# One-core encoder layer on Trainium2: full-tile operand sums go from GpSimd to VectorE, and the reciprocal roots become a multiply-add and a power on GpSimd

## The chip, the cores and the metric

The kernel runs on one core of one Trainium2 chip. The metric is the device time of one execution in microseconds (us). The engines of the core are named as in the profile: PE is TensorE (matrix products and transposes), DVE is VectorE, ACT is ScalarE, POOL is GpSimd, SP is SyncE, which issues most of the DMAs. Each engine works through its own list of instructions strictly in order.

## What is computed

One layer of an encoder on x of 1024 x 1024, float32. The parts that matter here, cut from the reference:

```python
h = rms_norm(x, g_mix)                       # x * rsqrt(mean(x*x) + eps) * g
z = h @ w_in                                 # queries, keys, values, index keys, gates
k_i = apply_rope(rms_norm(ik, g_idx_k))      # index keys; q_i has rope alone
y_a, y_b, y_c = band_attention, top-k sparse attention, gated recurrence
merged = sum over 3 branches of sigmoid(gate) * (y_branch @ w_branch)
x = x + merged @ w_out                       # out-projection
gu = rms_norm(x, g_ffn) @ w_ffn_in           # FFN-in
g_, u_ = split(gu)
x = x + (silu(g_) * u_) @ w_ffn_out          # FFN-out
```

Every product is made with float32 accuracy, so its operands are split in two parts, high and low.

## The kernel before

**Products.** `split` (L104 to L106) makes a high part with an ACT copy (L105) and the low part as raw minus high with a DVE subtraction (L106, names that end in l: `hl`, `ol`, `tql`, `fwl`). `mm3` (L121 to L123) then issues three matmuls: high by high, high by low, low by high. So a product can't finish before DVE has the low part of its operand.

**Seven products for eight.** The gate projection, the out-projection and both FFN products are made with a scheme that needs seven block products in place of eight. The price is sums and differences of operand blocks before the products. These are the full-tile operand sums of the change: 128x512 or 128x1024, two inputs in SBUF, output in SBUF. Before the change some of them stand on DVE and some on POOL:

- the index stage (about 20 to 90 us): `t2` of the rope on the queries, two 128x512 products on POOL for each half of the rows (L284, L285);
- the T stage (about 595 to 640 us), sums `tq` of the blocks of h for the gate projection: L796 to L800, of which two blocks of four (`ON_POOL`) and one low part are on POOL; the weights' sums of the same scheme are L872 to L875, and L889 adds two results;
- the comb stage (about 811 to 860 us), operand sums of the out-projection: L945 in `comb`, called from `o_prep`, 12 of 128x1024 on POOL, 4 on DVE;
- trans2 (about 920 to 947 us), sums of the normalised blocks for FFN-in: L1045 and L1047 on DVE, L1046 and L1048 on POOL;
- FFN-in (to about 1330 us): four 128x512 weight sums on POOL for each of 22 steps (L1169 to L1172).

**Reciprocal roots.** `rsqrt` (L125 to L140) makes 1/sqrt(scale * s + eps) on a narrow column by a bit trick and three Newton steps. It is 12 small instructions on DVE (the first norm in three batches, L184 to L187; the second norm, 8 tiles, L1002 to L1005) or 15 on POOL (index keys `rsk`, 128x4, twice, L274 to L278; heads of attention, `r16`, 128x16, eight times, L348 to L352).

**Order.** The Python code writes the work stage by stage, interleaved by hand (a string of letters decides which piece of attention comes between which products). The tile scheduler then sets the order of every engine's list by its own estimate of times, so moving an instruction to another engine also changes what stands around it. Loads for the FFN (`fa`, `fb`) are issued by SP; a load waits until the buffer that it overwrites is read for the last time. POOL also issues the DMAs that write intermediate results to DRAM.

```python
def split(raw, hi, lo, eng=None):
    S.activation(hi, raw, AF.Copy)
    (eng or V).tensor_tensor(lo, raw, hi.bitcast(F32), op=OP.subtract)
...
def comb(dst, a, op, b, eng=G):
    for o, x_, y_ in zip(dst, a, b):
        eng.tensor_tensor(o, x_, y_, op=op)
```

Of the kernel before, what the change touches and what calls it, by code (L numbers as in the profile page):

```python
# [20 lines left out]
D = 1024  # L21
# [14 lines left out]
ON_POOL = ('12', '21')  # L36
NPS = 0
# [45 lines left out]
def hybrid_kernel(ctx: ExitStack, tc: tile.TileContext, x, small, cs, bias_a, lru_w, w_idx, w_zg, w_c, w_g, w_b,  # L83
# [170 lines left out]
    for g in range(2):  # L254
# [29 lines left out]
        G.tensor_mul(t2[:, :, :, 0:32], zq[:, :, :, 32:64], bc(st[:, :, 0:32], 4))  # L284
        G.tensor_mul(t2[:, :, :, 32:64], zq[:, :, :, 0:32], bc(st[:, :, 32:64], 4))  # L285
# [115 lines left out]
    def attention(i, b0, pr, qk, v, mask, yT, isB=False):  # L401
# [4 lines left out]
        for e in range(2):  # L406
# [10 lines left out]
            (G if (b0 == 0 and isB and e < NPS) else V).tensor_scalar(P[:, 0:w], P[:, 0:w], rc, None, op0=OP.mult)  # L417
# [366 lines left out]
    def steps_T():  # L784
        tmp = Slots(arena, sl.free_list[:4])
        sl.free_list = sl.free_list[4:]
        for kp in range(2):
# [78 lines left out]
    def steps_W():  # L866
        for j in range(NPAIR):
# [21 lines left out]
            G.tensor_tensor(x, x, y, op=OP.add)  # L889
# [273 lines left out]
    def ffn_rest(j):  # L1163
# [313 lines left out]
```

## Time and profile before

| | us |
|---|---|
| median of 3 runs | 1560.23 (1556.93 to 1562.47) |
| the profiled execution, its time | 1559.64 |
| its span | 1557.9 |
| PE busy | 1485.1 (95%) |
| DVE busy | 1128.8 (72%) |
| ACT busy | 760.5 (49%) |
| POOL busy | 356.6 (23%) |

Busy shares are means over stages with different limits. In most of the span PE has no idle time; its roughly 70 us of idle time lie in a few stretches, and so the views by time (the windows, the timeline) tell more than the shares. In the timeline's rows a time in brackets is how long the engine was idle before the instruction and what ended that idle time. An instruction on DVE or POOL may show as busy while it waits for access to SBUF; its row is then longer than that of the same shape elsewhere.

### The profile page before, as it was taken

Reading aid. Unit: us, or ns where it says so; the run is one execution under the profiler, and the core shown is the slowest. Engines: PE = TensorE matmul, PEld = TensorE weight load, DVE = VectorE, ACT = ScalarE, POOL = GpSimd, SP = SyncE. Lnnn points to the kernel's source line nnn. Section 1 sums busy time; section 2 is a strip of 40 time slices with the busy share of each in tenths; the row PEclk is TensorE's granted clock in tenths of the full one; section 3 lists DMA queues with packets and bytes.
Section 4 is the critical chain, followed back from the end, with each engine's and each line's share of the span. In section 5 each row is a group of like instructions: output and inputs, shape, how many; then the busy total and the mean of one; then the engine's idle time right before and its main releaser. Section 6 shows DMA issues by size and latency. Waiting matters only on the chain. (4 is left out here: it accounts for less than half of the span.)

```text
span 1557.9 us, 20304 instructions
## 1 busy us (share of the span) xinstructions
PE 1485.1 (95%) x7612; PEld 1239.6 (80%) x7612; DVE 1128.8 (72%) x1932; ACT 760.5 (49%) x1188; POOL 356.6 (23%) x418
## 2 busy tenths in 40 slices
PE   6899989999999997999997988999999999999998
PEld 5888678889778875788885867888888888878887
DVE  5679999889666779748879887555555555378873
ACT  5455768865778665534213373333333333254440
POOL 1430001210000215542026153333333334000000
PEclk9999999999999999999998999999999999999999
DMA  4011212122111130348642231233333233598532
GB/s 173 28 45 42 68 37 88 57 82 78 54 45 55 41 109 28 135 155 291 231 152 105 95 109 41 95 108 103 114 96 113 98 121 117 217 360 293 187 128 88
DMA packets 51091, 178.43 MB, mean 115 GB/s; under 512 B 5872, under 2 KB 6000, under 8 KB 50992
## 3 DMA queue, kind: packets, MB, share of 16 engines
q1 hardware_dynamic: 36576, 128.36, 24.7%
q0 software_dynamic: 12688, 45.62, 7.5%
q10 hardware_dynamic: 1728, 3.15, 0.5%
q8 instruction: 60, 0.98, 0.3%
q14 instruction: 39, 0.32, 0.1%
HBM read 131.75 MB, written 45.35 MB: 114 GB/s over the span
## 5 line engine op out<-in xcount | busy, mean ns | idle before, releaser
L122 PE MATMUL B<-hl,fwh 128*128 128x512 f32 x528 | 207.1, 393 | 8.7 <-DVE hl L106 8.7
L121 PE MATMUL B<-hh,fwh 128*128 128x512 f32 x528 | 203.0, 391 | 1.6 <-ACT h2r L1023 1.6
L123 PE MATMUL B<-hh,fwl 128*128 128x512 f32 x528 | 199.7, 392 | 0.3 <-DVE fwl L106 0.3
L122 PEld LDWEIGHTS B<-hl,fwh 128*128 128x128 f32 x528 | 99.9, 189 | 30.7 <-DVE hl L106 10.0
L121 PEld LDWEIGHTS B<-hh,fwh 128*128 128x128 f32 x528 | 99.8, 189 | 22.7 <-ACT h2r L1023 1.8
L123 PEld LDWEIGHTS B<-hh,fwl 128*128 128x128 f32 x528 | 99.8, 189 | 21.2 <-DVE fwl L106 0.5
L122 PE MATMUL G<-wzl,hTh 128*128 128x256 f32 x384 | 111.0, 290 | 3.9 <-DVE wzl L106 3.9
L121 PE MATMUL G<-wzh,hTh 128*128 128x256 f32 x384 | 109.6, 287 | 2.0 <-ACT wzh L105 1.3
L123 PE MATMUL G<-wzh,hTl 128*128 128x256 f32 x384 | 110.0, 287 | 0.0
L122 PE MATMUL B<-fol,foh 128*128 128x512 f32 x264 | 102.8, 390 | 0.4 <-DVE fol L106 0.4
L123 PE MATMUL B<-foh,fol 128*128 128x512 f32 x264 | 101.9, 389 | 0.0
L121 PE MATMUL B<-foh,foh 128*128 128x512 f32 x264 | 101.1, 390 | 0.4 <-ACT foh L105 0.4
L106 DVE TENSOR_TENSOR fwl<-s,fwh 128x1024 fp32r<-128x1024 f32 x44 | 53.8, 1224 | 63.0 <-PE B L122 60.5
L660 ACT ACTIVATE junk_s<-score,ngS 128x1024 int8<-128x1024 f32 (+2 forms) x78 | 77.6, 995 | 21.1 <-DVE ngS L658 17.3
L122 PEld LDWEIGHTS G<-wzl,hTh 128*128 128x128 f32 x384 | 74.2, 193 | 5.4 <-DVE wzl L106 4.4
L123 PE MATMUL G<-hTh,wgl 128*128 128x512 f32 x192 | 76.3, 397 | 2.0 <-DVE wgl L106 2.0
L121 PEld LDWEIGHTS G<-wzh,hTh 128*128 128x128 f32 x384 | 74.0, 194 | 3.7 <-ACT wzh L105 1.7
L121 PE MATMUL G<-hTh,wgh 128*128 128x512 f32 x192 | 76.7, 400 | 0.0
L122 PE MATMUL G<-hTl,wgh 128*128 128x512 f32 x192 | 75.9, 395 | 0.0
L1188 DVE TENSOR_TENSOR act<-act,B 128x512 f32<-128x512 f32 x22 | 15.1, 688 | 82.2 <-PE B L123 82.2
L123 PEld LDWEIGHTS G<-wzh,hTl 128*128 128x128 f32 x384 | 74.3, 193 | 0.4 <-issue 0.2
L105 ACT ACTIVATE fw<-fb 128x512 fp32r<-128x512 f32 x22 | 13.9, 634 | 123.0 <-PE B L123 121.7
(499 smaller groups left out, 4146.1 us busy)
## 6 DMA issues: line engine op xcount, KB each, us to landing
fw<-in_w_fo SPq DMA_DIRECT2D x33, 512.0 KB, 5.9
fa<-pd SPq DMA_DIRECT2D x33, 512.0 KB, 5.0
gl<-gd SPq DMA_DIRECT2D x24, 512.0 KB, 5.8
fa<-in_w_fi SPq DMA_DIRECT2D x22, 512.0 KB, 3.5
fb<-in_w_fi SPq DMA_DIRECT2D x22, 512.0 KB, 3.9
pd<-act POOLq DMA_DIRECT2D x22, 512.0 KB, 6.1
ga<-in_w_g SPq DMA_DIRECT2D x18, 512.0 KB, 3.6
x<-in_x SPq DMA_DIRECT2D x12, 512.0 KB, 4.4
```

What stands on the lines that cost most here:

```text
L105: S.activation(hi, raw, AF.Copy)
L106: (eng or V).tensor_tensor(lo, raw, hi.bitcast(F32), op=OP.subtract)
L121: PE.matmul(o, lhsT=lh, rhs=rh, start=first, stop=False, **kw)
L122: PE.matmul(o, lhsT=lh, rhs=rl, start=False, stop=False, **kw)
L123: PE.matmul(o, lhsT=ll, rhs=rh, start=False, stop=last, **kw)
L660: S.activation(junk_s[:, 0:(i + 1) * 128], score[i], AF.Sign, bias=self.ng.bitcast(F32)[:, j:j + 1], accum_out=self.cnt[:, j:j + 1])
L1188: V.tensor_add(a1, a1, x)
```

## The change

It does three things. All the sums listed above, and the low part of T1, go from POOL to DVE. `rsqrt` becomes two POOL instructions, a multiply-add and a power with the exponent -0.5, for all its callers, those that had it on DVE too. The switches that no longer decide anything are taken out. The columns' exponents come from a 128x16 constant that DVE fills once. POOL's list goes from 417 to 162 instructions; the rest are DMAs, tables and memsets. In the changed file the lines up to `rsqrt` stand 2 lower, and those behind it 10 to 12 lower (L106 is L104, L796 is L784, L945 is L933, L1045 is L1033).

```diff
-    def rsqrt(dst, src, n, scale, eng=None):
-        E = G if eng is None else eng
+    mhalf = const.tile([128, 16], F32, name="mhalf")
+    V.memset(mhalf, -0.5)
+
+    def rsqrt(dst, src, n, scale):
         v = const.tile([128, n], F32, name="rs_v", tag=f"rsv{n}", bufs=2)
...
-        E.tensor_scalar(v, src, scale, EPS, op0=OP.mult, op1=OP.add)
-        E.tensor_scalar(y.bitcast(I32), v.bitcast(I32), -0.5, float(0x5F3759DF), op0=OP.mult, op1=OP.add)
-        E.tensor_scalar(v, v, -0.5, None, op0=OP.mult)
-        for it in range(3):
-            E.tensor_tensor(t, y, y, op=OP.mult)
-            E.tensor_tensor(t, t, v, op=OP.mult)
-            if E is V:
-                V.scalar_tensor_tensor(dst if it == 2 else y, t, 1.5, y, op0=OP.add, op1=OP.mult)
-            else:
-                G.tensor_scalar(t, t, 1.5, None, op0=OP.add)
-                G.tensor_tensor(dst if it == 2 else y, t, y, op=OP.mult)
+        G.tensor_scalar(v, src, scale, EPS, op0=OP.mult, op1=OP.add)
+        G.tensor_tensor(dst, v, mhalf[:, 0:n], op=OP.pow)
...
-        rsqrt(rs_x[:, t0:t0 + tn], ss_x[:, t0:t0 + tn], tn, 1.0 / D, V)
+        rsqrt(rs_x[:, t0:t0 + tn], ss_x[:, t0:t0 + tn], tn, 1.0 / D)
...
-        G.tensor_mul(t2[:, :, :, 0:32], zq[:, :, :, 32:64], bc(st[:, :, 0:32], 4))
-        G.tensor_mul(t2[:, :, :, 32:64], zq[:, :, :, 0:32], bc(st[:, :, 32:64], 4))
+        V.tensor_mul(t2[:, :, :, 0:32], zq[:, :, :, 32:64], bc(st[:, :, 0:32], 4))
+        V.tensor_mul(t2[:, :, :, 32:64], zq[:, :, :, 0:32], bc(st[:, :, 32:64], 4))
...
-                    E = (G if nm in ON_POOL else V)
-                    E.tensor_tensor(q[nm][:, i], hi, lo, op=OP.add)
+                    V.tensor_tensor(q[nm][:, i], hi, lo, op=OP.add)
...
-                split(q[src], *tq[name, kp], G if name == "T1" else V)
+                split(q[src], *tq[name, kp])
...
-            G.tensor_tensor(s12[:, 0], b[:, 0], b[:, 1], op=OP.add)
+            V.tensor_tensor(s12[:, 0], b[:, 0], b[:, 1], op=OP.add)
...
-            G.tensor_tensor(x, x, y, op=OP.add)
+            V.tensor_tensor(x, x, y, op=OP.add)
...
-    def comb(dst, a, op, b, eng=G):
+    def comb(dst, a, op, b, eng=V):
...
-            rsqrt(rs2[:, t:t + 1], ss2[:, t:t + 1], 1, 1.0 / D, V)
+            rsqrt(rs2[:, t:t + 1], ss2[:, t:t + 1], 1, 1.0 / D)
...
-            G.tensor_tensor(b12, b22, b12, op=OP.subtract)
+            V.tensor_tensor(b12, b22, b12, op=OP.subtract)
             V.tensor_sub(t2, b22, b11)
-            G.tensor_tensor(b21, b21, t2, op=OP.subtract)
+            V.tensor_tensor(b21, b21, t2, op=OP.subtract)
...
-        G.tensor_tensor(s12[:, 0], b[:, 0], b[:, 1], op=OP.add)
-        G.tensor_tensor(s12[:, 1], s12[:, 0], a[:, 0], op=OP.subtract)
-        G.tensor_tensor(s34[:, 0], a[:, 0], b[:, 0], op=OP.subtract)
-        G.tensor_tensor(s34[:, 1], a[:, 1], s12[:, 1], op=OP.subtract)
+        V.tensor_tensor(s12[:, 0], b[:, 0], b[:, 1], op=OP.add)
+        V.tensor_tensor(s12[:, 1], s12[:, 0], a[:, 0], op=OP.subtract)
+        V.tensor_tensor(s34[:, 0], a[:, 0], b[:, 0], op=OP.subtract)
+        V.tensor_tensor(s34[:, 1], a[:, 1], s12[:, 1], op=OP.subtract)
```

The order of DVE's list in the index stage, second half of the rows before, at the place where the scaled index keys `zk` wait for `rsk` (`zq` are the index queries, `hTl` the low part of the transposed input, `qi` the stacked queries):

```order
L286 TENSOR_TENSOR zq_328<-zq_328,cs_319 128x1024
L200 SCALAR_TENSOR_TENSOR hTl_92<-S,sm,hTh_91 128x512
L287 TENSOR_TENSOR zq_328<-zq_328,t_36_469 128x1024
L200 SCALAR_TENSOR_TENSOR hTl_96<-S,sm,hTh_95 128x512
L278 SCALAR_TENSOR_TENSOR zk_329<-zk_329,rsk,sm 128x64
L200 SCALAR_TENSOR_TENSOR hTl_94<-S,sm,hTh_93 128x512
L278 SCALAR_TENSOR_TENSOR zk_329<-zk_329,rsk,sm 128x64 x3
```

and the same place in the changed kernel:

```order
L273 TENSOR_TENSOR t_36_420<-zq_294,cs_285 128x16x32
L274 TENSOR_TENSOR t_36_420<-zq_294,cs_285 128x16x32
L189 SCALAR_TENSOR_TENSOR hTl_88<-S,sm,hTh_87 128x512
L263 TENSOR_REDUCE ssk<-sq_408 128x4
L275 TENSOR_TENSOR zq_294<-zq_294,cs_285 128x1024
L189 SCALAR_TENSOR_TENSOR hTl_92<-S,sm,hTh_91 128x512
L189 SCALAR_TENSOR_TENSOR hTl_94<-S,sm,hTh_93 128x512
L276 TENSOR_TENSOR zq_294<-zq_294,t_36_420 128x1024
L267 SCALAR_TENSOR_TENSOR zk_295<-zk_295,rsk,sm 128x64 x4
```

Two rope products (L273, L274) have come onto DVE ahead of the scaling by `rsk`, and the four scalings now stand together, with no `hTl` between them.

DVE's list in the comb stage, from the last gated sums of the branches (L981; `m` are these sums, `s` and `t` operand sums, `wo` blocks of the weight, `ol` low parts, `x` the residual), before:

```order
L945 TENSOR_TENSOR s_7833<-m_7151,m_7461 128x1024
L945 TENSOR_TENSOR s_7834<-m_7303,m_7643 128x1024
L981 TENSOR_TENSOR m_7644<-m_7644,mt_7780 128x512
L106 TENSOR_TENSOR ol_7838<-s_7833,oh_7837 128x1024
L106 TENSOR_TENSOR ol_7842<-s_7834,oh_7841 128x1024
L945 TENSOR_TENSOR s_7833<-s_7833,m_7152 128x1024
L945 TENSOR_TENSOR s_7834<-s_7834,m_7304 128x1024
L1105 SCALAR_TENSOR_TENSOR x_418_7807<-B,x_418_7807 128x512
L1105 SCALAR_TENSOR_TENSOR x_419_7809<-B,x_419_7809 128x512
L106 TENSOR_TENSOR ol_7918<-s_7833,oh_7917 128x1024
```

and in the changed kernel:

```order
L933 TENSOR_TENSOR s_7649<-m_6967,m_7277 128x1024
L933 TENSOR_TENSOR s_7650<-m_7119,m_7459 128x1024
L969 TENSOR_TENSOR m_7460<-m_7460,mt_7596 128x512
L933 TENSOR_TENSOR m_6967<-m_6968,m_6967 128x1024
L104 TENSOR_TENSOR ol_7654<-s_7649,oh_7653 128x1024
L933 TENSOR_TENSOR m_7119<-m_7120,m_7119 128x1024
L104 TENSOR_TENSOR ol_7658<-s_7650,oh_7657 128x1024
L933 TENSOR_TENSOR s_7649<-s_7649,m_6968 128x1024
L1093 SCALAR_TENSOR_TENSOR x_418_7623<-B,x_418_7623 128x512
L1093 SCALAR_TENSOR_TENSOR x_419_7625<-B,x_419_7625 128x512
L933 TENSOR_TENSOR s_7650<-s_7650,m_7120 128x1024
```

The differences of the `m` blocks, which stood on POOL, now stand between DVE's own sums and the low parts. Further on the sums of `t` and `wo` stand between low parts in the same way: from the first row of this place to the low part of the first `t`, DVE has 18 instructions of 128x1024 and 9 of 128x512 in the changed kernel.

DVE's list in trans2 (`h2r` are the normalised blocks, `hl` their low parts, `s`, `fw` and `fwl` weights of FFN-in, `gx` FFN-in's first results), before:

```order
L106 TENSOR_TENSOR fw_8788<-fb_8772,fw_8788 128x512
L1005 TENSOR_SCALAR xn_8542<-x_421_7813,rs_7824 128x1024
L106 TENSOR_TENSOR fwl_8865<-fa_8862,fwh_8864 128x1024
L1160 TENSOR_TENSOR gx_8641<-gx_8641,B 128x512
L1045 TENSOR_TENSOR h2r_8305<-h2r_8670,h2r_8305 128x1024
L1047 TENSOR_TENSOR t_478_8722<-h2r_8683,h2r_8305 128x1024
L106 TENSOR_TENSOR hl_8740<-h2r_8683,hh_8739 128x1024
L106 TENSOR_TENSOR hl_8736<-h2r_8305,hh_8735 128x1024
```

and in the changed kernel:

```order
L1159 TENSOR_TENSOR s_9_8620<-fa_8355,fb_8617 128x512
L1157 TENSOR_TENSOR s_8_8619<-fb_8617 128x512
L1158 TENSOR_TENSOR s_8_8619<-s_8_8619,fa_8355 128x512
L1160 TENSOR_TENSOR s_9_8620<-fa_8355,s_8_8619 128x512
L104 TENSOR_TENSOR fwl_8585<-fa_8582,fwh_8584 128x1024
L1148 TENSOR_TENSOR gx_8361<-gx_8361,B 128x512
L1033 TENSOR_TENSOR h2r_8073<-h2r_8390,h2r_8073 128x1024
L1034 TENSOR_TENSOR h2r_8390<-h2r_8403,h2r_8390 128x1024
L1035 TENSOR_TENSOR t_478_8442<-h2r_8403,h2r_8073 128x1024
L104 TENSOR_TENSOR hl_8456<-h2r_8073,hh_8455 128x1024
L104 TENSOR_TENSOR hl_8460<-h2r_8403,hh_8459 128x1024
```

The four weight sums of an FFN step (L1157 to L1160) stand on DVE ahead of this stage's first difference, and L1034, which was on POOL, between L1033 and L1035. From L1033 to the last low part of the stage DVE has 18 instructions of 128x1024 and one of 128x512.

## Rows read from the trace of the kernel before

**Rows 1.** The page, part 1: busy time of each engine, share, instructions.

```profile
PE 1485.1 (95%) x7612; PEld 1239.6 (80%) x7612; DVE 1128.8 (72%) x1932; ACT 760.5 (49%) x1188; POOL 356.6 (23%) x418
```

**Rows 2.** Waits of PE: waiting engine and line, releaser: total us, times, longest.

```profile
PE S L197 <- DVE x L187: 12.3, 1, 12.3
PE B L122 <- DVE hl L106: 8.7, 3, 3.6
PE B L122 <- DVE ol L106: 8.6, 2, 6.7
PE T L431 <- ACT PT L424: 7.3, 5, 6.2
...
PE G L123 <- DVE hTl L200: 2.8, 2, 1.8
```

**Rows 3.** Windows of comb, trans2 and FFN-in: PE, PEld, DVE, ACT, POOL, granted clock.

```profile
836.00:848.00 12.00, 5.85 (x15) 4.64 (x16) 12.00 (x10) 3.19 (x4) 10.66 (x4) 0.57 0.00 0
936.00:948.00 12.00, 9.00 (x25) 6.86 (x26) 12.00 (x10) 5.48 (x7) 3.02 (x1) 0.72 0.00 1
960.00:1320.00 360.00, 360.00 (x1590) 298.09 (x1589) 203.76 (x211) 125.03 (x173) 124.28 (x108) 1.00 0.31 104
```

**Rows 4.** Timeline of DVE: start us, busy us, operation. Behind the comb sums.

```profile
847.67 1.27 DVE L1105 SCALAR_TENSOR_TENSOR x<-B,x 128x512 f32<-128x512 f32 x2
848.86 1.21 DVE L106 TENSOR_TENSOR ol<-wo,oh 128x1024 fp32r<-128x1024 f32 x1
```

**Rows 5.** Timeline of DVE at the start, root and first scaled x.

```profile
9.12 0.17 DVE L130 TENSOR_SCALAR rs_v<-ss_x 128x2 f32<-128x2 f32 x1 [5.82 <-ACT junk L184]
...
11.36 1.42 DVE L187 TENSOR_SCALAR x<-x,rs_x 128x1024 f32<-128x1024 f32 x2
```

**Rows 6.** Timeline of DVE in the index stage, both waits for the root.

```profile
48.84 0.28 DVE L278 SCALAR_TENSOR_TENSOR zk<-zk,rsk,sm 128x64 f32<-128x64 f32 x1 [2.62 <-POOL rsk L140]
...
73.35 0.87 DVE L278 SCALAR_TENSOR_TENSOR zk<-zk,rsk,sm 128x64 f32<-128x64 f32 x4 [2.71 <-POOL rsk L140]
```

**Rows 7.** Timeline of POOL in the index stage, the second root, its ends.

```profile
65.08 0.39 POOL L130 TENSOR_SCALAR rs_v<-ssk 128x4 f32<-128x4 f32 x1
...
73.12 0.20 POOL L140 TENSOR_TENSOR rsk<-rs_t,rs_y 128x4 f32<-128x4 f32 x1
```

**Rows 8.** Timeline of ACT in the T stage, high parts and PT.

```profile
606.44 1.06 ACT L105 ACTIVATE tqh<-tq 128x1024 fp32r<-128x1024 f32 x1 [5.30 <-DVE tq L798]
607.40 0.96 ACT L424 ACTIVATE PT<-T 128x512 f32<-128x512 f32 x2
```

**Rows 9.** Timeline of DVE in the T stage.

```profile
601.31 2.21 DVE L797 TENSOR_TENSOR tq<-tq,tq 128x1024 f32<-128x1024 f32 x1
```

**Rows 10.** Timeline of DVE in the comb stage.

```profile
811.02 2.35 DVE L945 TENSOR_TENSOR s<-m,m 128x1024 f32<-128x1024 f32 x2
...
838.74 3.35 DVE L106 TENSOR_TENSOR ol<-t,oh 128x1024 fp32r<-128x1024 f32 x1
```

**Rows 11.** Timeline of POOL in the comb stage.

```profile
837.70 3.31 POOL L945 TENSOR_TENSOR t<-wo,t 128x1024 f32<-128x1024 f32 x1
```

**Rows 12.** Timeline of ACT ahead of trans2.

```profile
919.10 1.06 ACT L105 ACTIVATE fwh<-s 128x1024 fp32r<-128x1024 f32 x1 [3.42 <-POOL s L1170]
...
920.59 2.40 ACT L1023 ACTIVATE h2r<-B,sm 128x512 f32<-128x512 f32 x4
```

**Rows 13.** Timeline of DVE in trans2.

```profile
921.86 1.23 DVE L1045 TENSOR_TENSOR h2r<-h2r,h2r 128x1024 f32<-128x1024 f32 x1 [3.35 <-ACT h2r L1023]
...
946.84 1.21 DVE L106 TENSOR_TENSOR fwl<-s,fwh 128x1024 fp32r<-128x1024 f32 x1
```

**Rows 14.** Timeline of POOL in the W stage and in FFN-in, sums behind loads.

```profile
687.87 1.29 POOL L872 TENSOR_TENSOR s<-ga 128x512 f32<-128x512 f32 x1 [9.25 <-DMA ga<-in_w_g]
...
1133.24 1.27 POOL L1171 TENSOR_TENSOR s<-fa,fb 128x512 f32<-128x512 f32 x1 [3.56 <-DMA fb<-in_w_fi]
```

**Rows 15.** Waits of DVE, columns as above: heads that wait for POOL's root.

```profile
DVE zB L352 <- POOL r L140: 4.7, 3, 3.8
```

More of the change, by code (lines that the diff above doesn't have):

```diff
@@ L35 @@
 TILES = ((6, 3, 2, 4), (7, 5, 4))
-ON_POOL = ('12', '21')
-NPS = 0
 YL = 3
@@ L123, in mm3 @@
         PE.matmul(o, lhsT=ll, rhs=rh, start=False, stop=last, **kw)
-    def rsqrt(dst, src, n, scale, eng=None):
-        E = G if eng is None else eng
+    mhalf = const.tile([128, 16], F32, name="mhalf")
+    V.memset(mhalf, -0.5)
+    def rsqrt(dst, src, n, scale):
         v = const.tile([128, n], F32, name="rs_v", tag=f"rsv{n}", bufs=2)
-        y = const.tile([128, n], F32, name="rs_y", tag=f"rsy{n}", bufs=2)
-        t = const.tile([128, n], F32, name="rs_t", tag=f"rst{n}", bufs=2)
-        E.tensor_scalar(v, src, scale, EPS, op0=OP.mult, op1=OP.add)
-        E.tensor_scalar(y.bitcast(I32), v.bitcast(I32), -0.5, float(0x5F3759DF), op0=OP.mult, op1=OP.add)
-        E.tensor_scalar(v, v, -0.5, None, op0=OP.mult)
-        for it in range(3):
-            E.tensor_tensor(t, y, y, op=OP.mult)
-            E.tensor_tensor(t, t, v, op=OP.mult)
-            if E is V:
-                V.scalar_tensor_tensor(dst if it == 2 else y, t, 1.5, y, op0=OP.add, op1=OP.mult)
-            else:
-                G.tensor_scalar(t, t, 1.5, None, op0=OP.add)
-                G.tensor_tensor(dst if it == 2 else y, t, y, op=OP.mult)
+        G.tensor_scalar(v, src, scale, EPS, op0=OP.mult, op1=OP.add)
+        G.tensor_tensor(dst, v, mhalf[:, 0:n], op=OP.pow)
     ps = tc.tile_pool(name="ps", bufs=1, space=PSUM)
@@ L416, in attention @@
             V.reciprocal(rc, sm_)
-            (G if (b0 == 0 and isB and e < NPS) else V).tensor_scalar(P[:, 0:w], P[:, 0:w], rc, None, op0=OP.mult)
+            V.tensor_scalar(P[:, 0:w], P[:, 0:w], rc, None, op0=OP.mult)
             pt_s = sl.get((128, 8, 128), F32, "PT")
@@ L794, in steps_T @@
                     hi, lo = (a[:, 512 * half:512 * half + 512].bitcast(F32) for a in hT[k0 + 2 * kp + i])
-                    E = (G if nm in ON_POOL else V)
-                    E.tensor_tensor(q[nm][:, i], hi, lo, op=OP.add)
+                    V.tensor_tensor(q[nm][:, i], hi, lo, op=OP.add)
             V.tensor_sub(q["11"], q["12"], q["11"])
-            (G if "T3" in ON_POOL else V).tensor_tensor(q["12"], q["22"], q["12"], op=OP.subtract)
+            V.tensor_tensor(q["12"], q["22"], q["12"], op=OP.subtract)
             V.tensor_sub(q["22"], q["22"], q["11"])
-            (G if "T4" in ON_POOL else V).tensor_tensor(q["21"], q["21"], q["22"], op=OP.subtract)
+            V.tensor_tensor(q["21"], q["21"], q["22"], op=OP.subtract)
             for name, src in (("T2", "22"), ("T3", "12"), ("T1", "11"), ("T4", "21")):
                 tq[name, kp] = (sl.get((128, 2, 512), F32R, "tqh"), sl.get((128, 2, 512), F32R, "tql"))
-                split(q[src], *tq[name, kp], G if name == "T1" else V)
+                split(q[src], *tq[name, kp])
                 tmp.free(q[src])
@@ L1058, in o_prep @@
         if n == "5":
-            comb(ss, A21, OP.add, A22, V)
+            comb(ss, A21, OP.add, A22)
         elif n == "6":
             comb(ts, b22, OP.subtract, ts)
-            comb(ss, ss, OP.subtract, A11, V)
+            comb(ss, ss, OP.subtract, A11)
         elif n == "4":
@@ L1168, in ffn_rest @@
         s34 = rr.get((128, 2, 4, 128), F32, "s34")
-        G.tensor_tensor(s12[:, 0], b[:, 0], b[:, 1], op=OP.add)
-        G.tensor_tensor(s12[:, 1], s12[:, 0], a[:, 0], op=OP.subtract)
-        G.tensor_tensor(s34[:, 0], a[:, 0], b[:, 0], op=OP.subtract)
-        G.tensor_tensor(s34[:, 1], a[:, 1], s12[:, 1], op=OP.subtract)
+        V.tensor_tensor(s12[:, 0], b[:, 0], b[:, 1], op=OP.add)
+        V.tensor_tensor(s12[:, 1], s12[:, 0], a[:, 0], op=OP.subtract)
+        V.tensor_tensor(s34[:, 0], a[:, 0], b[:, 0], op=OP.subtract)
+        V.tensor_tensor(s34[:, 1], a[:, 1], s12[:, 1], op=OP.subtract)
         w12 = split_w(s12, 2)
```

## The prediction, made before the changed kernel was run

> **What bounds the kernel now.** I read the page first: PE is busy 1485.1 us of a span of 1557.9 [rows 1], so about 73 us is all that a change which leaves the matmuls alone can take out by closing gaps; what the clock costs comes on top. The list of PE's waits says who owns that time [rows 2]: 12.3 us at the start for DVE's first scaled x, 8.7 us in trans2 for low parts `hl`, 8.6 us in the comb stage for `ol` (one wait of 6.7), 7.3 us around the T stage for PT (one of 6.2), 2.8 us in the index stage for `hTl`. The windows by stage come next [rows 3]. In FFN-in PE is busy 360.00 of 360.00 us and the clock is granted in full, so nothing that DVE or POOL does there sets the end. In 836 to 848 us (comb) PE is busy 5.85 of 12 us and DVE 12.00 of 12.00; in 936 to 948 us (trans2) PE 9.00 and DVE 12.00. In these two the mean granted clock is 0.57 and 0.72: after each gap PE ran for some us at 1.2 in place of 2.4 GHz, which counts as busy. The kernel is thus bound by PE, but in comb and trans2 by DVE.
>
> Why is DVE late there? A low part `ol` of 128x1024 takes 1.21 us where no POOL sum runs [rows 4], and 3.35 us at 838.74 [rows 10] beside a POOL sum of 3.31 us that began at 837.70 [rows 11]. It ends 1.08 us behind the POOL sum: the two seem to take turns, not to share. In the sums that follow, the price of a DVE instruction is its distance to the next, not its busy time: two 128x512 are 1.19 us apart from the next row, so 0.60 each [rows 4]; two 128x1024 are busy 2.35 us [rows 10] where one alone is 1.21, so 1.14 each.
>
> **Comb, -5 us.** From 811.02 until the first `ol` from `t` ends, at 838.74 + 3.35 = 842.09 us, before takes 31.1 us [rows 10]. The order of the changed kernel has 18 instructions of 128x1024 and 9 of 128x512 in that stretch: 18 x 1.14 + 9 x 0.60 = 25.9 us. DVE gets more instructions, but none that waits for POOL, and the low part comes at about 837, 5 us earlier. PE's 6.7 us gap shrinks by that; the half clock behind it may go as well, which I leave to the range.
>
> **Trans2, -7 us.** ACT waits 3.42 us for the weight sum of POOL (L1170) before `fwh`, and the copies `h2r` stand behind that, at 920.59 [rows 12]. With the sum on DVE, at 0.60 us each and right behind the load, I take the copies at 917, which is 3.6 us earlier; PE was not idle then, so this is the softest number. DVE waited 3.35 us for the copies and began 1.27 us after their first [rows 12, 13]. From there to the last `hl` it has 18 x 1.14 + 0.60 = 21.1 us of work: 917 + 1.3 + 21.1 = 939.4 us. Before, the weight part `fwl` that follows the last `hl` starts at 946.84 [rows 13]: 7.4 us, taken as 7. If the copies don't come earlier it is 4.
>
> **T stage, -4 us.** ACT's high part at 606.44 had waited 5.30 us for DVE's L798, and the copies PT that PE needs stand behind it at 607.40 [rows 8]. Ahead of L798, DVE's L797 took 2.21 us at 601.31 [rows 9] where the price alone is 1.14, and the L796 sums beside POOL's likewise. In the changed order ACT's copies PT stand ahead of that high part, so the 6.2 us gap should shrink to about half (-3), and the later low parts come earlier (-1). DVE has more to do: 8 x 0.60 + 2 x 1.14 = 7.1 us; so the range here is 0 to -7.
>
> **Index stage, -3 us.** DVE waits twice for `rsk`, 2.62 and 2.71 us [rows 6]; POOL's chain for the second runs from 65.08 to 73.32, 8.2 us [rows 7]. Two instructions replace 15, so the waits go, and for each half two rope products of 0.60 us come onto DVE. That is 1.4 to 1.5 us earlier for each half, about 3 in all, with gaps of PE behind both (the first is in the 2.8 us of `hTl` [rows 2]).
>
> **Start, -1 us.** The 12 DVE instructions last from 9.12 to 11.36 us, 2.24 us, with nothing beside them, and PE's first wait of 12.3 us ends behind them [rows 2, 5]. In their place stand a multiply-add and a power on POOL. No row shows a power. The nearest row is POOL's product of 128x4, 0.20 us [rows 7]; two of these with a handoff each way would be under 1 us (-1.4). The other end is a full chain like the 8.2 us one, +6. I take 1.2 us, nearest to the plain product, because the column has only 2 elements to a row.
>
> **W stage, +1 us.** POOL waits 9.25 us at 687.87 for a weight load [rows 14], and that costs only itself. On DVE the same sum, at the head of the list, holds low parts and result sums queued behind it that PE needs soon. From 0 to +3; I take +1.
>
> **FFN-in, 0.** 88 sums x 0.60 = 53 us come to DVE, which is busy 203.76 of 360 us [rows 3]; even if nothing comes back, that is 257 of 360. PE's 100% there covers it. What could break the cover is order: POOL waits 3.56 us for the load `fb` [rows 14], and on DVE this wait would hold the low parts behind it. But the load is released by the step's last sum, which comes earlier on DVE; I count on that margin. If it failed at all 22 steps by 1 us it would be +22.
>
> **The rest, 0.** The heads' roots on POOL cost DVE waits of 4.7 us in the list of DVE's waits (its longest 3.8) [rows 15]; PE had other work there. The scheduler writes a new order from 20 to 580 us; that can go either way by some 4 us.
>
> **Sum:** -1 - 3 - 4 + 1 - 5 - 7 = -19 us. The profiled execution took 1559.64 us, 0.6 below the median of 1560.23, so 1559.64 - 19 = 1540.6; I say **1541**.
>
> **Rivals.**
> A, *all port waits and clock losses vanish.* PE's waits for `hl`, `ol` and PT are 24.6 us [rows 2], and the clock in the two windows cost about 5.85 x 0.43 + 9.00 x 0.28 = 5 us [rows 3]; with 1 + 3 us of the start and the index stage and 1 us of W it is 33 us: about 1527. Against it: DVE's own work in these stages only shrinks from 31.1 to 25.9 us and the like.
> B, *DVE is the bound anyway.* If the long rows mostly covered time in which DVE would have waited for ACT's high parts or PE's banks, the comb and trans2 terms fall to 2 us each and T to 0: 1559.64 - 1 - 3 + 1 - 4 = about 1553.
> C, *the new order eats it.* Same sum, but the rewritten list from 20 to 580 us, or loads on DVE in W and FFN-in, cost some 15 us: about 1557 to 1560.
> D, *slower: the power is long on POOL.* It stands on the path of 8 heads with 128x16, where DVE works in order behind it. The old chain of 15 is the cover, 8.2 us on 128x4 [rows 7]. At P us for a power the price is 8 x (P - 8.2); the 19 us are gone at P = 10.6, and at 12.5 us it is +34, so 1541 + 34 = 1575.
> E, *slower: DVE's rows are long for reasons of its own.* If the 3.35 us at 838.74 don't fall, every moved sum in the DVE-bound stages adds itself: comb 12 x 1.14, trans2 4 x 1.14 + 4 x 0.60, T with four W sums 7.1 + 2.4 us; together 30 us, so 1559.64 + 30 - 4 = about 1586. It decides where a moved sum costs more than the other rows fall. Against it: the 1.21 us rows come exactly where POOL is idle [rows 4].
> The Trainium skill, "Perfetto Trace Analysis", section "Optimizing Scalar/DVE Operations", says that where DVE is saturated it may make sense to offload work to GpSimd; DVE is saturated in comb and trans2, and by that rule this change, which takes the offloading back, would end as in E. The same paragraph warns that the two share a read port and that moving work between them might not help; the rows of 3.31 and 3.35 us side with the warning.
>
> **How the numbers follow.** About 0.3% (4.7 us) is what a measurement can tell from no change, so faster means below 1555.5 and slower above 1564.9. Chances: the forecast 0.62 (1530 to 1549, all faster), A 0.07 (faster), B 0.13 (half of it at the near edge of no change: 0.07 faster, 0.06 same), C 0.08 (same 0.07, slower 0.01), D 0.07 and E 0.03 (slower). Faster 0.76, same 0.13, slower 0.11. The range is from 1530, where the clock comes back in one stage and T gives its 7, to 1557, B with some of C; it leaves out A, D, E and the upper part of C.
>
> **What would show it.** Right: in the changed kernel's timeline every DVE row of 128x1024 from SBUF is near 1.2 us; the first `ol` from `t` ends about 26 us after the first L933; the last `hl` some 21 us after L1033; no wait of DVE for `rsk`; the first PE matmul near 11.3 us; PE still at 100% in FFN-in. Wrong: a power of several us, waits of DVE for loads `ga` or `fb` with idle time of PE behind them, DVE rows still over 2 us, or new gaps of PE between 100 and 580 us that have the size of those closed.

## The result and the profile after

The changed kernel takes 1543.55 us in the median of 4 runs (1538.80 to 1546.76), the kernel before 1560.33 us beside it; the ratio is 0.9892, with an interval from 0.986 to 0.9924. Run once more, unaltered, beside the experiments below, it takes 1540.61 us (0.9873, from 0.9858 to 0.9887). The forecast was 1541, the range 1530 to 1557. The profiled execution of after took 1538.80 us, 20.8 less than that of before, and is the lowest of its four.

The first line of the page of after answers to [rows 1]. PE loses little busy time, DVE is about as busy as before, though 148 sums and low parts of POOL have come to it (130 of 128x512 and 18 of 128x1024, some 98 us at 0.60 and 1.14), and POOL is almost empty:

```profile
PE 1479.5 (96%) x7612; PEld 1237.1 (80%) x7612; DVE 1119.4 (73%) x1949; ACT 760.7 (49%) x1188; POOL 108.4 (7%) x162
```

PE's waits in the kernel after, which answer to [rows 2] (waiting engine and line, releaser: total us, times, longest):

```profile
PE S L186 <- DVE x L176: 11.2, 1, 11.2
PE B L120 <- DVE ol L104: 4.7, 2, 2.9
PE B L119 <- ACT hh L103: 3.3, 2, 2.8
PE B L120 <- DVE hl L104: 3.2, 2, 2.5
...
PE T L412 <- ACT yA L422: 2.7, 2, 1.7
PE S L526 <- DVE us L207: 2.6, 3, 1.4
...
PE T L420 <- ACT PT L413: 1.1, 4, 0.5
...
PE G L121 <- DVE hTl L189: 1.0, 1, 1.0
```

The waits for `ol` and `hl` fall from 17.3 to 7.9 us, that for PT at L431 (L420 now) from 7.3 to 1.1. New are 3.3 us for the high parts `hh` of ACT. Grown are the waits at L412 for `yA` and at L526 for `us`, in the middle of the program: 2.7 and 2.6 us, 0.2 and 0.8 before.

Where did it go, stage by stage? I took the moments at which PE starts the same product in both traces; the difference of two moments' lead is what the stage between them gained. (S, T and B are PSUM names; a negative number is a gain.)

| stage, and the product that ends it | before | after | lead | stage | predicted |
|---|---|---|---|---|---|
| start: first transpose of x | 12.26 | 11.17 | -1.1 | -1.1 | -1 |
| index: last product of the index scores | 114.54 | 106.98 | -7.6 | -6.5 | -3 |
| attention, heads, recurrence: first product of the gate projection | 534.93 | 531.74 | -3.2 | +4.4 | 0 |
| T: last `hh` by `gw` product of the first group | 645.93 | 635.08 | -10.9 | -7.7 | -4 |
| W and branches: first product of the out-projection | 811.16 | 799.44 | -11.7 | -0.9 | +1 |
| comb: first product of FFN-in | 904.44 | 888.00 | -16.4 | -4.7 | -5 |
| trans2: first product by `fw` on its results | 956.22 | 934.34 | -21.9 | -5.4 | -7 |
| FFN-in: its last such product | 1345.63 | 1323.75 | -21.9 | 0 | 0 |
| FFN-out: its last product | 1553.45 | 1532.40 | -21.1 | +0.8 | 0 |

One trace gives a single stage only roughly. The changed kernel run again has -5.0 us in the index stage, +2.1 in the next and -7.0 in trans2; two variants below with the same code in the index stage (FFN's sums back on GpSimd, the old chain for the heads) have -3.1 and -4.2 there, and -4.2 both in trans2. T and comb agree better: in these four traces T gains 7.5 to 8.7 us and comb 4.7 to 4.9.

The windows of after around the largest remaining gaps of comb and trans2, and in FFN-in, answer to [rows 3] (PE, PEld, DVE, ACT, POOL, granted clock):

```profile
819.00:831.00 12.00, 9.14 (x34) 7.04 (x33) 12.00 (x16) 4.85 (x5) 0.00 (x0) 0.86 0.00 0
831.00:843.00 12.00, 10.15 (x38) 7.88 (x37) 12.00 (x14) 5.33 (x6) 0.00 (x0) 0.86 0.00 0
914.00:926.00 12.00, 6.73 (x20) 4.94 (x21) 10.91 (x11) 5.84 (x8) 0.00 (x0) 0.72 0.00 0
940.00:1300.00 360.00, 360.00 (x1590) 298.10 (x1589) 214.33 (x289) 125.53 (x173) 18.72 (x35) 1.00 0.30 103
```

DVE is still the full engine in comb (12.00 of 12), but PE is busy 9.14 us of 12 with a mean granted clock of 0.86, where it was 5.85 and 0.57. The next 12 us are at 0.86 too, where those behind the window of before were at 1.00. The half clock (1.2 GHz) thus costs PE as much in comb as before, by its busy time times one minus the clock 1.3 + 1.4 us against 2.5: what comb gained is idle time. The window of trans2 holds its largest gaps and so says little by itself. Over the whole stages of the table, comb and trans2 before and then after:

```profile
811.16:904.44 93.28, 83.56 (x368) 67.98 (x369) 88.11 (x144) 41.03 (x50) 37.25 (x19) 0.95 0.29 106
904.44:956.22 51.78, 40.87 (x176) 32.11 (x175) 45.25 (x57) 28.90 (x39) 27.44 (x14) 0.93 0.22 70
```

```profile
799.44:888.00 88.56, 83.85 (x368) 68.50 (x369) 76.39 (x87) 41.60 (x51) 10.44 (x21) 0.96 0.30 112
888.00:934.34 46.34, 39.78 (x179) 31.66 (x178) 38.86 (x43) 28.37 (x38) 1.93 (x4) 0.93 0.23 76
```

PE's idle time falls from 9.7 to 4.7 us in comb and from 10.9 to 6.6 us in trans2.

In FFN-in PE is busy 360.00 of 360 us, though DVE now has 78 more instructions in that window (289, 211 before), some 47 us at 0.60. Its busy time rises from 203.76 to 214.33 us only, so most of what came is paid for by shorter rows of the others.

DVE in the comb stage after, the first row and the low part of the first `t`, answers to [rows 10]:

```profile
799.31 2.35 DVE L933 TENSOR_TENSOR s<-m,m 128x1024 f32<-128x1024 f32 x2
...
824.00 1.21 DVE L104 TENSOR_TENSOR ol<-t,oh 128x1024 fp32r<-128x1024 f32 x1
```

From 799.31 to 824.00 + 1.21 = 825.21 are 25.9 us, the number that the prediction had counted; before it was 31.1. No DVE row between is longer than 1.3 us to an instruction.

The start: POOL's two instructions and DVE's first x, which answer to [rows 5]; then the prices of the power on POOL by its columns (engine, operation, shapes, count, busy us, mean ns):

```profile
9.32 0.19 POOL L128 TENSOR_SCALAR rs_v<-ss_x 128x2 f32<-128x2 f32 x1 [4.40 <-ACT junk L173]
9.59 0.73 POOL L129 TENSOR_TENSOR rs_x<-rs_v,mhalf 128x2 f32<-128x2 f32 x1
```

```profile
10.36 1.42 DVE L176 TENSOR_SCALAR x<-x,rs_x 128x1024 f32<-128x1024 f32 x2 [7.14 <-POOL rs_x L129]
```

```profile
L129 POOL TENSOR_TENSOR r<-rs_v,mhalf 128x16 f32<-128x16 f32 x8 | 23.8, 2978 | 0.7
...
L129 POOL TENSOR_TENSOR rs<-rs_v,mhalf 128x1 f32<-128x1 f32 x8 | 4.8, 602 | 0.7
```

From the last input to the first x are 1.04 us with handoffs (9.32 to 10.36), where 1.2 was taken. A power takes 0.60 us for one column and 2.98 for 16. That is far below the 10.6 us from which rival D decides. (Its cover of 8.2 us was read from a chain on 128x4; the eight chains on 128x16 of the kernel before take 4.5 to 7.8 us, and the power is below these too.)

The index stage after, DVE's scaling by `rsk` (both halves), answers to [rows 6]:

```profile
44.33 0.86 DVE L267 SCALAR_TENSOR_TENSOR zk<-zk,rsk,sm 128x64 f32<-128x64 f32 x4
...
65.82 0.87 DVE L267 SCALAR_TENSOR_TENSOR zk<-zk,rsk,sm 128x64 f32<-128x64 f32 x4 [0.90 <-POOL rsk L129]
```

The wait of 2.62 us is gone and that of 2.71 is 0.90.

ACT and DVE around trans2 after, which answer to [rows 12, 13]:

```profile
900.05 1.83 ACT L1011 ACTIVATE h2r<-B,sm 128x512 f32<-128x512 f32 x3
```

```profile
901.33 1.23 DVE L1033 TENSOR_TENSOR h2r<-h2r,h2r 128x1024 f32<-128x1024 f32 x1 [0.59 <-ACT h2r L1011]
...
923.42 1.23 DVE L104 TENSOR_TENSOR fwl<-s,fwh 128x1024 fp32r<-128x1024 f32 x1 [0.43 <-PE B L120]
```

### The profile page after: what moved, and what is told of

Same layout as the page of the kernel before. It is cut to its first block, busy times and chain, and to the rows that moved or that the text cites. A ratio compares the mean times of both kernels' runs of the same rounds, so it can differ in the third digit from the quotient of the medians.

```text
span 1536.8 us, 19968 instructions
## 1 busy us (share of the span) xinstructions
PE 1479.5 (96%) x7612; PEld 1237.1 (80%) x7612; DVE 1119.4 (73%) x1949; ACT 760.7 (49%) x1188; POOL 108.4 (7%) x162
## 4 chain that ended last, share of the span: by engine, by line
PE 63%; DVE 7%; ACT 3%; DMA 2%; issue 1%; SPq 0%; DVEq 0%; ACTq 0%
PE B L120 14%; PE B L121 14%; PE B L119 14%; PE G L121 4%; PE G L119 4%; PE G L120 4%; PE T L120 1%; PE T L119 1%; PE T L121 1%; PE S L119 1%; DMA fa<-pd 1%; PE S L121 1%; PE S L120 1%; PE T L420 1%; DVE ol L104 1%
## 5 line engine op out<-in xcount | busy, mean ns | idle before, releaser
L104 DVE TENSOR_TENSOR fwl<-s,fwh 128x1024 fp32r<-128x1024 f32 x44 | 53.9, 1225 | 78.2 <-PE B L120 77.4
L649 ACT ACTIVATE junk_s<-score,ngS 128x1024 int8<-128x1024 f32 (+2 forms) x78 | 77.5, 993 | 17.3 <-DVE ngS L647 13.1
L103 ACT ACTIVATE foh<-fa 128x1024 fp32r<-128x1024 f32 x33 | 35.0, 1060 | 58.7 <-DMA fa<-pd 38.2
```

What stands on the lines that cost most here:

```text
L649: S.activation(junk_s[:, 0:(i + 1) * 128], score[i], AF.Sign, bias=self.ng.bitcast(F32)[:, j:j + 1], accum_out=self.cnt[:, j:j + 1])
```

## The experiments

**The roots alone, and the sums alone.** The two halves of the change, each by itself. The first leaves all sums where they were:

```diff
-    def rsqrt(dst, src, n, scale, eng=None):
+    def rsqrt(dst, src, n, scale):
...
+        G.tensor_scalar(v, src, scale, EPS, op0=OP.mult, op1=OP.add)
+        G.tensor_tensor(dst, v, mhalf[:, 0:n], op=OP.pow)
```

> The kernel before with the reciprocal roots alone changed (multiply-add and power on GpSimd, for all callers); all operand sums stay where they were. In the changed kernel's trace a power took 0.60 us on 128x1, 0.73 on 128x2, 1.01 on 128x4 and 2.98 on 128x16. Theory 1 (roots and sums act in their own stages): -1 us at the start, -4 to -6 in the index stage, some us back between 285 and 490 us if the heads' new roots are what rewrote the order there; comb, T and trans2 as before; in all -2 to -6 us, and the wait of 6.2 us for PT and of 6.7 us for ol stay. Theory 2 (most of the gain is the order that the scheduler writes anew, whatever moves): T, comb and trans2 change here too, by 5 us or more in one of them.

Measured: 1557.47 us against 1560.34, ratio 0.9983 (0.9974 to 0.9992), -2.9 us. The waits of PE for DVE and ACT in the late stages stay:

```profile
PE B L122 <- DVE hl L106: 9.3, 4, 5.9
PE B L122 <- DVE ol L106: 8.6, 2, 6.7
PE T L422 <- ACT PT L415: 6.7, 3, 6.1
```

By stages it gains 1.3 us at the start, 5.7 in the index stage and 2.6 in trans2; T gains nothing (+0.9) and comb nothing (+0.1). So the new order that the roots bring does not make the gains of T and comb. But between the index stage and the gate projection it gives back 5.6 us.

The second is the changed kernel with the old roots:

```diff
...
+        rsqrt(rs_x[:, t0:t0 + tn], ss_x[:, t0:t0 + tn], tn, 1.0 / D, V)
...
+            rsqrt(rs2[:, t:t + 1], ss2[:, t:t + 1], 1, 1.0 / D, V)
```

> The changed kernel with the old reciprocal roots (12 instructions on VectorE at the start and in the second norm, 15 on GpSimd for index keys and heads); all sums on VectorE. Theory 1: T, W, comb and trans2 gain as in the changed kernel, -8, -1, -5 and -3 to -5 us, the start nothing and the index stage 0 to -3: -13 to -18 us in all against the kernel before. If the 8 us that the changed kernel gave back between 285 and 490 us come from the roots, they aren't lost here and the time is up to 8 us lower. Theory 2: less than -8 us.

Measured: 1540.82 us, ratio 0.9875 (0.9861 to 0.9889), -19.5 us; index -2.6, T -8.6, W -0.9, comb -5.5, trans2 -3.2. In the middle it gives nothing back (-0.4). It is as fast as the whole change (1543.55 and 1540.61), so the roots together add nothing on top of the sums, though alone they lead by 6.9 us at 115 us.

**The sums of comb and trans2 alone.**

```diff
-    def comb(dst, a, op, b, eng=G):
+    def comb(dst, a, op, b, eng=V):
...
-            G.tensor_tensor(b12, b22, b12, op=OP.subtract)
+            V.tensor_tensor(b12, b22, b12, op=OP.subtract)
...
-            G.tensor_tensor(b21, b21, t2, op=OP.subtract)
+            V.tensor_tensor(b21, b21, t2, op=OP.subtract)
```

> The kernel before with only the sums of the comb stage and of trans2 on VectorE (12 and 4 of 128x1024). The order up to 800 us stays. Theory 1 (VectorE and GpSimd take turns at SBUF): the VectorE rows of 3.3 us in these stages fall to 1.2, the wait of 6.7 us for ol to 2 to 3; -5 us in comb and -3 to -5 in trans2: -8 to -10 us. Theory E of the prediction (rows long for reasons of their own): 18 to 20 us slower.

Measured: 1553.46 us, ratio 0.9953 (0.9939 to 0.9967), -6.9 us, somewhat less than expected. Comb gained 5.6 us and trans2 1.7; PE's longest wait for `ol` is 2.9 us. Some 2.5 us were given back at the beginning of FFN-out, where PE waits 2.2 us for a high part `foh`; why there, these runs don't show. Rival E (18 to 20 us slower) is out.

**GpSimd's sums made narrow.** Here DVE's work, the count of instructions and their waits stay as before, and only the length of POOL's sums is taken away. This leaves out most of their result. (The expectation says 11 of 12 sums of comb; it is 10 of 12, all but the two of the first pair, and the 4 of trans2.)

```diff
-    def comb(dst, a, op, b, eng=G):
+    def comb(dst, a, op, b, eng=G, a_=None):
         for o, x_, y_ in zip(dst, a, b):
+            if eng is G and dst is not a_:
+                o, x_, y_ = (z[:, :, 0:8] for z in (o, x_, y_))
             eng.tensor_tensor(o, x_, y_, op=op)
...
-            comb(ts, b12, OP.subtract, b11)
+            comb(ts, b12, OP.subtract, b11, a_=ts)
...
-            G.tensor_tensor(b12, b22, b12, op=OP.subtract)
+            G.tensor_tensor(b12[:, :, 0:8], b22[:, :, 0:8], b12[:, :, 0:8], op=OP.subtract)
...
-            G.tensor_tensor(b21, b21, t2, op=OP.subtract)
+            G.tensor_tensor(b21[:, :, 0:8], b21[:, :, 0:8], t2[:, :, 0:8], op=OP.subtract)
```

> The kernel before with GpSimd's sums of comb (11 of 12, all but the first pair's two) and of trans2 made on 16 of 1024 columns only, so most of their result is left out; VectorE's work, the number of instructions and all waits between them stay. If the two engines take turns, VectorE's rows in these stages fall to 1.2 us, comb and trans2 end earlier by more than with the sums on VectorE (the work is gone from both): -8 us and -7 us, about -15 us in all. If VectorE's rows are long for reasons of their own, they stay at 2 to 3.4 us and the time changes by less than 4 us.

Measured: 1537.51 us, ratio 0.9855 (0.9843 to 0.9868), -22.8 us, more than the 15 expected: comb gained 13.3 us and trans2 9.0, and PE waits for `ol` no more and for `hl` 1.2 us in all. DVE's rows in comb, in the stretch of [rows 10]: first one of before, then those of this run.

```profile
816.10 4.55 DVE L106 TENSOR_TENSOR ol<-s,oh 128x1024 fp32r<-128x1024 f32 x2
```

```profile
814.43 2.37 DVE L106 TENSOR_TENSOR ol<-s,oh 128x1024 fp32r<-128x1024 f32 x2
...
826.63 1.24 DVE L106 TENSOR_TENSOR ol<-t,oh 128x1024 fp32r<-128x1024 f32 x1
```

Two `ol` from `s` take 2.37 us where they took 4.55, and the first `ol` from `t`, 3.35 us before, takes 1.24. DVE has the same instructions, in another order at a few places from the last of these on; so its long rows were time in which POOL's sums held it up. That the sums' results come earlier can't be the reason, since DVE had no idle time in this stretch before. That is the mechanism of the prediction, shown by itself. It also tells what moving the sums leaves on the table in comb, some 8 us: the sums' work on DVE, by which PE in the changed kernel still has 4.7 us of idle time there and the half clock that goes with it.

**The T stage's sums alone.** Here the prediction was too small by half.

```diff
-ON_POOL = ('12', '21')
+ON_POOL = ()
...
-                split(q[src], *tq[name, kp], G if name == "T1" else V)
+                split(q[src], *tq[name, kp])
```

> The kernel before with only the T stage's sums and the low part of T1 on VectorE (8 of 128x512 and 2 of 128x1024); everything else as before, and the order up to 580 us too. In ACT's list four copies PT now stand ahead of the first high part. The changed kernel gained 7.6 to 8.6 us here where 4 were predicted. Theory 1 (both act: taking turns at SBUF, and the high part that held PT): -7 to -9 us, the wait of 6.2 us for PT gone. If the gain of the T stage needed the weights' sums of the W stage too, -3 to -5 us.

Measured: 1553.59 us, ratio 0.9963 (0.995 to 0.9975), -6.1 us, and by the trace -7.7 in the T stage. The longest wait for PT is 0.5 us.

**The T stage's sums on GpSimd, narrow.** ACT's order stays that of before, with the high part ahead of the copies PT; most of 8 sums is left out.

```diff
-                    E.tensor_tensor(q[nm][:, i], hi, lo, op=OP.add)
+                    w = 8 if E is G else 512
+                    if E is G:
+                        G.memset(q[nm][:, i, w:512], 1.0)
+                    E.tensor_tensor(q[nm][:, i, 0:w], hi[:, 0:w], lo[:, 0:w], op=OP.add)
```

> The kernel before with GpSimd's 8 sums of the T stage made on 8 of 512 columns; the rest of these tiles is filled with a constant by GpSimd, which reads nothing from SBUF; most of these sums is left out. VectorE's work, the low part of T1 on GpSimd and ACT's order (the high part ahead of PT) stay. Theory 1a (mainly turns at SBUF): VectorE's L797 comes down from 2.2 to 1.2 us and the high part about 4 us earlier, so the 6.2 us wait falls to 2 to 3 and the stage gains 5 to 8 us in all. Theory 1b (mainly ACT's order): the wait stays at 5 to 6 us, and the gain is 2 to 3 us, from the later low parts.

Measured: 1553.59 us, ratio 0.996 (0.9946 to 0.9973), -6.1 us, and by the trace -7.5 in the T stage. ACT's high part and PT, and the wait of PE, which answer to [rows 8] and [rows 2]:

```profile
603.86 1.06 ACT L105 ACTIVATE tqh<-tq 128x1024 fp32r<-128x1024 f32 x1 [1.96 <-DVE tq L801]
604.82 0.96 ACT L424 ACTIVATE PT<-T 128x512 f32<-128x512 f32 x2
```

```profile
PE T L431 <- ACT PT L424: 3.7, 4, 2.9
```

The high part waits 1.96 us instead of 5.30 and PE's longest wait for PT falls from 6.2 to 2.9 us with ACT's order unchanged. So taking turns at SBUF is enough for the gain of this stage (theory 1a). What ACT's new order adds can't be told from these two runs, since the sums' own work is on DVE in one and left out in the other.

**FFN's sums back on GpSimd.**

```diff
-        V.tensor_tensor(s12[:, 0], b[:, 0], b[:, 1], op=OP.add)
+        G.tensor_tensor(s12[:, 0], b[:, 0], b[:, 1], op=OP.add)
...
-        V.tensor_tensor(s34[:, 1], a[:, 1], s12[:, 1], op=OP.subtract)
+        G.tensor_tensor(s34[:, 1], a[:, 1], s12[:, 1], op=OP.subtract)
```

> The changed kernel with the 88 weight sums of FFN-in back on GpSimd. The prediction counted this part at 0, since PE has no idle time there: 1540 to 1546 us, PE at 100% from 960 to 1300 us, VectorE rows of 1.2 and 0.68 us back at up to 1.8 where they meet a sum. If these sums' move mattered, through loads or trans2, it is slower by 3 us or more; the sums at the end of trans2 may cost 1 to 3 us.

Measured: 1540.86 us, ratio 0.9875 (0.9861 to 0.9888), beside 1540.61 for the changed kernel: no difference. The window of FFN-in (columns as above) and one DVE row in it:

```profile
940.00:1300.00 360.00, 360.00 (x1590) 298.20 (x1589) 203.24 (x211) 124.56 (x172) 124.19 (x108) 1.00 0.31 104
```

```profile
1101.65 1.82 DVE L1182 TENSOR_TENSOR act<-act,gx 128x512 f32<-128x512 f32 x1
```

A product of 128x512 is held up to 1.82 us again, and PE is still busy 360.00 of 360 us. 88 of the 148 moved instructions are worth nothing to the time.

**What was given back in the middle.** The changed kernel, run again as the standard:

> The changed kernel once more, unaltered, as the standard for the runs beside it and for a second trace: 1539 to 1547 us, with some 6 to 9 us of idle time and half clock of PE between 280 and 500 us, as in the first trace (8.6 against 1.8 before).

The changed kernel with the old chain for the heads alone, then its counterpart with the power for the heads alone:

```diff
-        rsqrt(r16, s16, 16, 1.0 / 64)
+        rsqrt_n(r16, s16, 16, 1.0 / 64)
```

> The changed kernel with the old chain of 15 on GpSimd for the heads alone (128x16, eight times); the other roots keep multiply-add and power. In the order that results the transposes of zB stand where the kernel before has them, ahead of the gated recurrence's products; with the power they stand 166 places later in PE's list. Theory O (the 8 us given back between 285 and 500 us are the new order around the heads): they come back, and the time is that of the sums alone less 1 us at the start, 4 to 5 in the index stage and 2 in trans2: 1533 to 1537 us, below the changed kernel by 6 to 9. Theory S (PE's early gain is swallowed by VectorE's top-k search, which is busy to 95% from 100 to 300 us, whatever the order): no difference, 1540 to 1545 us.

```diff
-        rsqrt(rs_x[:, t0:t0 + tn], ss_x[:, t0:t0 + tn], tn, 1.0 / D)
+        rsqrt_n(rs_x[:, t0:t0 + tn], ss_x[:, t0:t0 + tn], tn, 1.0 / D, V)
...
-        rsqrt(rsk, ssk, 4, 1.0 / 64)
+        rsqrt_n(rsk, ssk, 4, 1.0 / 64)
...
-            rsqrt(rs2[:, t:t + 1], ss2[:, t:t + 1], 1, 1.0 / D)
+            rsqrt_n(rs2[:, t:t + 1], ss2[:, t:t + 1], 1, 1.0 / D, V)
```

> The counterpart: multiply-add and power for the heads alone, the old chains for the first norm, the index keys and the second norm; all sums on VectorE. The order around the heads is that of the changed kernel. Theory O: 5 to 8 us slower than the sums alone (1540.8), 1546 to 1549 us, idle time of PE between 280 and 500 us as in the changed kernel. Theory S: there is no early gain to swallow, so it is like the sums alone, 1539 to 1543 us.

Measured on one chip: the changed kernel 1540.61 us (1537.84 to 1542.57, 4 runs), with the old chain for the heads 1534.17 us (1532.36 to 1535.81, 5 runs; ratio 0.9829, from 0.9816 to 0.9842), with the power for the heads only 1544.16 us (1540.30 to 1545.39, 5 runs; 0.9894, from 0.988 to 0.9908). The intervals of the first two don't overlap: with the power for the heads the kernel is 6.4 us slower, as theory O has it, and theory S, which expected no difference, falls. (The profiled executions, 1537.84 and 1535.81 us, are the lowest of one set and the highest of the other, so the traces show less of it.) The counterpart lies 3.3 us above the sums alone (another chip; 5 to 8 were expected), with overlapping intervals, so it only leans the same way: 1544.16 us is in neither theory's range.

The windows from 280 to 500 us of the changed kernel run again, of the kernel with the old chain for the heads, of before, and of the kernel with the power for the heads only (the columns as above):

```profile
280.00:500.00 220.00, 214.00 (x1279) 180.77 (x1278) 161.55 (x289) 156.44 (x250) 15.55 (x18) 1.00 0.18 58
```

```profile
280.00:500.00 220.00, 218.26 (x1318) 185.55 (x1318) 164.16 (x291) 157.52 (x248) 17.74 (x44) 1.00 0.18 58
```

```profile
280.00:500.00 220.00, 218.20 (x1314) 184.82 (x1313) 166.93 (x309) 157.31 (x257) 18.35 (x45) 1.00 0.19 63
```

```profile
280.00:500.00 220.00, 215.60 (x1286) 181.75 (x1286) 163.89 (x298) 157.72 (x256) 15.55 (x18) 1.00 0.18 60
```

PE is idle 6.0 us there with the power, 1.7 with the chain, 1.8 before, and 4.4 with the power for the heads only. The other traces divide the same way: the five with the heads' power have 4.4 to 6.1 us, the seven without it 1.6 to 2.0. The waits in question, of the changed kernel run again and then with the chain (whose lines stand 17 lower):

```profile
PE S L526 <- DVE us L207: 2.7, 3, 1.4
...
PE G L119 <- ACT ge L544: 1.6, 2, 1.1
...
PE T L412 <- ACT yA L422: 1.0, 1, 1.0
```

```profile
PE S L543 <- DVE us L224: 0.9, 1, 0.9
...
PE G L119 <- ACT ge L561: 0.5, 1, 0.5
```

(With the chain PE waits for `yA` too, 1.7 us, but outside this stretch, at 196 us.) These waits are for the recurrence's input `us` and for ACT's reads of PSUM into `ge` and `yA`. None of these is a root. What the roots changed is the order: with the heads' power the scheduler puts the first transposes of `zB` 166 places later in PE's list (places 2240 and 2074 of the traces' matmuls, counted from 0), and between the recurrence's first product (place 2248 in both) and the first product of `us` stand 108 other matmuls with the power, 126 without. So PE comes to `us` sooner, and waits. That the order is the cause, and the whole of the 6.4 us, is inferred, not shown: no run here has the one order with the other root. The power itself is not slow there: 2.98 us on 128x16, where the eight chains in the kernel with the old one take 4.5 to 8.0 us (the shortest from 300.97 to 305.42). The lead by PE's products agrees: with the chain the kernel keeps its 6.0 us from 115 to 535 us to a tenth, and the changed kernel run again goes from 6.5 over 9.7 (at 282 us) back to 4.4.

The version with the old chain for the heads, 1534.17 us, beats both kernels.

## Why the prediction was right, and where its terms were off

**Comb (-5, measured -4.7).** The count 18 x 1.14 + 9 x 0.60 = 25.9 us came out as 25.9. The half clock, left to the range, did not come back here. Moving work onto the engine that bounds the stage paid since each sum costs it 1.14 us there and cost it up to 2.1 us of waiting (3.35 less 1.21) before.

**Trans2 (-7, measured -5.4, and -7.0 in the second trace).** Measured from the first product of FFN-in, ACT's first copy comes at 12.05 us, 16.15 before: 4.1 us earlier, 3.6 were taken. DVE's first weight part behind the last `hl` comes at 35.4 us, 42.4 before: 7.0 earlier, as forecast. PE could not use it all. In its place PE now waits 3.3 us for ACT's high parts `hh`, a wait that the prediction didn't name. The runs also divide this term: the sums alone give 1.7 to 3.2 us, the second norm's roots 2.6.

**T (-4, measured -7.7).** The step that failed is its size. I let the wait for PT shrink by half and 1 us for the low parts. The wait went from 6.2 to 0.5 us, and PE's half clock behind it, which had cost some 2 us, went too; with the POOL sums narrow and ACT's order kept, the stage still gains 7.5. The bound of -7 that the range used was just passed. The half clock before, and the clock in the same place after:

```profile
604.00:613.00 9.00, 4.96 (x38) 4.42 (x38) 8.20 (x8) 5.45 (x9) 2.22 (x2) 0.62 0.00 0
```

```profile
600.00:610.00 10.00, 9.86 (x93) 8.04 (x94) 9.93 (x12) 7.12 (x12) 0.53 (x1) 1.00 0.12 30
```

**Index (-3, measured -6.5, and -5.0 in the second trace).** The waits for `rsk` shrank as forecast (2.62 to 0, 2.71 to 0.90). The size was off because I counted DVE's lead only; with PE's gaps its stretch at half clock went, which was worth 2.7 us from 60 to 120 us before (PE's busy time in the windows times one minus the clock: 8.02 us at 0.66 from 80 to 90 us) and is 0 after. The -3.1 and -4.2 us of the two other traces with this stage's code show that part of this excess is the scatter of single traces.

**The rest (0 with 4 us either way, measured +4.4, and +2.1 in the second trace).** Here is the one step that failed in kind. I looked at the heads' roots for what POOL and DVE do, and found cover, rightly. I named the scheduler's new order, but as something that goes either way, and did not tie it to the roots. With the heads' power PE is idle 4.4 to 6.1 us between 280 and 500 us, without it 1.6 to 2.0, most likely by the list of PE, which the scheduler wrote anew because an instruction off PE's path had another length. One of the prediction's own signs of being wrong, new gaps of PE between 100 and 580 us, thus showed in part. It took back 4.4 of the 7.6 us gained before 115 us (2.1 of 6.5 in the second trace).

**Start, W, FFN (-1, +1, 0; measured -1.1, -0.9, 0 and +0.8).** As forecast, W with the other sign; but its -0.9 shows in the kernel with the roots alone too, whose W sums stay on GpSimd, so it is not the gain of these sums. 0 for the FFN sums was tested and holds. The terms of the table add up to -21.1 at the last product, where -19 was forecast; the errors of T and index (-7.2) and those of the middle, trans2 and FFN-out (+6.8) nearly cancel. That the total was nearer than its parts was luck; what was not luck are the mechanism and the count in comb.

The Trainium skill, "Perfetto Trace Analysis", section "Optimizing Scalar/DVE Operations", says that where DVE is saturated, offloading some work to ScalarE or even GpSimd may make sense; taking the offloading back would then have made this kernel slower. The same paragraph warns that the two share an SBUF read port, so that this might not help, and the runs side with the warning: a low part of 1.21 us took 3.35 beside a GpSimd sum, and the sums alone moved to VectorE took the kernel from 1560.34 to 1540.82 us.

## What to carry to other kernels

Before you move an element-wise sum to GpSimd because VectorE is full, look at VectorE's rows of the same shape with and without a GpSimd sum beside them; if 1.21 us becomes 3.35, the sum costs VectorE more on GpSimd than on itself. Only the stages in which PE waits for VectorE count: here 88 of the moved sums were worth nothing. And when a scheduler writes the order, a shorter instruction can also mean a new order elsewhere; try each part of a change by itself, since a part that looks free can take back the gain of another.

## What the runs showed of the hardware

A power on GpSimd takes 0.60, 0.72, 1.02 and 2.98 us on 1, 2, 4 and 16 columns of 128 partitions, about 0.16 us for each column; on 16 columns it is shorter than the chain of 15 (4.5 to 8.0 us). Turns go both ways: the same power on 128x4 took 1.01 us at 42.10 and 3.53 us at 62.26, beside VectorE instructions with two SBUF inputs (62.56 and 63.70, 1.22 us each):

```profile
42.10 1.01 POOL L129 TENSOR_TENSOR rsk<-rs_v,mhalf 128x4 f32<-128x4 f32 x1
...
62.26 3.53 POOL L129 TENSOR_TENSOR rsk<-rs_v,mhalf 128x4 f32<-128x4 f32 x1
```

```profile
62.56 1.22 DVE L104 TENSOR_TENSOR wzl<-wzr,wzh 128x1024 fp32r<-128x1024 f32 x1
63.70 1.22 DVE L276 TENSOR_TENSOR zq<-zq,t 128x1024 f32<-128x1024 f32 x1
```

And with POOL's sums gone, VectorE's 128x1024 instructions in the changed kernel's comb are 1.13 to 1.14 us apart without exception from 799.31 to 846.94 us; I had not expected the count to hold to 0.1 us in 26.
